# Input projection of a decoder step as seven block products over pairs of weight chunks, with intermediates in device memory

## The chip, the cores and the metric

The kernel runs on one core of one Trainium2 chip. Its engines are TensorE (PE, matrix products into PSUM), VectorE (DVE), ScalarE (ACT), GpSimd (POOL, which doesn't reach PSUM) and SyncE (SP, which here issues every DMA). Each engine works through a queue of its own in program order. The metric is the time of one execution on the device, in microseconds; less is better.

## The reference

One layer of a decoder trunk for a prompt of 1024 tokens and 8 sample tokens (1032 together), width 1024:

```
h = x * (1 + scale(c)) + shift(c)
z = h @ w_in                       # 1024 x 8704: 68 chunks of 128 columns
q, k, v, g_att | cb, cc, cx, g_conv | cu, cv, g_chunk | merge = split(z)
A = rms_norm(diff_attention(q, k, v)) * silu(g_att)       # 4 heads; samples attend to a paged cache
B = cb * conv3(cc * cx) * silu(g_conv)
C = cu * (tril(W_s) @ layer_norm(cv) + b) * silu(g_chunk)
sub = (sum_n sigmoid(merge_n) * (branch_n @ w_branch_n)) @ w_out
y = layer_norm(alpha * x + gate(c) * sub)
```

Outputs are y, the new keys and values, the tail of the convolution's input, and the normalised cv rows of the samples.

## The kernel before

Everything is kept transposed: channels on the 128 partitions, the 1032 tokens along the free axis. Each fp32 operand is held as two float32r parts, hi (a rounded copy, made by ACT) and lo (the remainder src - hi, made by DVE or POOL), and a product is three matmuls: hi*hi, hi*lo, lo*hi.

`gemm` (L235) makes one chunk of z: for each of three units of 344 tokens, 8 blocks of k times 3 matmuls go into one PSUM bank, and `evac` then takes the bank away. 

```python
for u, (a, b) in enumerate(UNITS):                 # L238: 3 units of 344 tokens
    for k in range(nk):                            # nk = 8 for z, 4 for a branch projection
        mm(ps[:, :n], wh, xh[k][:, a:b], k == 0, False)
        mm(ps[:, :n], wh, xl[k][:, a:b], False, False)
        mm(ps[:, :n], wl, xh[k][:, a:b], False, k == nk - 1)
    evac(u, a, b, ps[:, :n])
    tick()                                         # one more step of every background generator
```

`w_load` (L183) fetches weights as half chunks (128 x 512) and `w_split` (L194) splits each; the lo part goes to POOL during attention (`lo_eng[0] = pool`, L846) and to DVE from the merge of branch B on (L909). The rest of the model runs as Python generators that emit a few instructions at every `tick`, so that one instruction stream interleaves them with the projection: `attention(h)` (L384, one head each), `decode_k` (L668, scores of the samples over 128 cached pages of keys: POOL multiplies a 128x1024 tile `kp` by the query at L723, DVE sums it at L710 into `Sdec`), `decode_v` (L774, PE sums the 128 pages of values), `chunk_side` (L942), `rms` (L1057), `ada_gate` (L1095).

The order written out by hand is: `startup` (L577), where h arrives block by block and the chunks q, k, v of head 0 accumulate over k; for each head q, k, v and the four convolution chunks beside that head's attention; then the gates and projections of branch B beside `decode_k`; the chunk-mixing chunks; the gates and projections of branch C beside `decode_v`; the gates of branch A, g_att; the projections of branch A; the output projection (`out`). All activations stay in SBUF, in 43 slots of 128x1032.

Of the kernel before, what the change touches and what calls it, by code (L numbers as in the profile page):

```python
# [16 lines left out]
P = 128  # L17
# [5 lines left out]
UNITS = [(0, 344), (344, 688), (688, 1032)]  # L23
H = 4
# [40 lines left out]
def step_kernel(ctx, tc, cT, sm, sn, lamb, xT, x_p, x_s, ada, adag, bgate, w_in, w_br, w_out, lnb,  # L65
# [3 lines left out]
    NS = 43  # L69
    spool = ctx.enter_context(tc.tile_pool(name="S", bufs=NS))  # L70
    wpool = ctx.enter_context(tc.tile_pool(name="W", bufs=4))
    upool = ctx.enter_context(tc.tile_pool(name="U", bufs=4))
    cpool = ctx.enter_context(tc.tile_pool(name="C", bufs=1))
    mpool = ctx.enter_context(tc.tile_pool(name="M", bufs=4))
    pz = ctx.enter_context(tc.tile_pool(name="PZ", bufs=3, space=PSUM))
    px = ctx.enter_context(tc.tile_pool(name="PX", bufs=5, space=PSUM))
# [12 lines left out]
    def utile(name, dt=F32):  # L89
        return upool.tile([P, 344], dt, tag="U", name=name)  # L90
# [6 lines left out]

    active = []
    later = []

    def tick():
        todo, later[:] = later[:], []
        for f in todo:
            f()
        for g in list(active):
            try:
                next(g)
            except StopIteration:
                active.remove(g)

    def pause(n):
        for _ in range(n):
            yield
# [31 lines left out]
    kS = cpool.tile([P, H, NB], F32, name="kS")  # L145
    convo = cpool.tile([P, 4, 18], F32, name="convo")
    chko = cpool.tile([P, 4, NB], F32, name="chko")
    vS = cpool.tile([P, H, NB], F32, name="vS")
    pt = cpool.tile([1, NB * PAGES], I32, name="pt")

# [1 line left out]
    wseq = []  # L152

    def want(kind, c):
        wseq.extend([(kind, c, 0), (kind, c, 1)] if kind == "z" else [(kind, c, 0)])

    wseq.extend([("s", c, r) for r in range(2) for c in (C_Q, C_K, C_V)])
    for h in range(H):
        for b in (C_Q, C_K, C_V, C_CC, C_CX, C_GC, C_CB)[0 if h else 3:]:
            want("z", b + h)  # L160
    for n in (1, 2):
        if n == 2:
            for b in (C_CV, C_CU, C_GU):
                for g in range(4):
                    want("z", b + g)
        for d in range(KD):
            want("z", C_M + 8 * n + d)
            want("b", 8 * n + d)
    for c in (*range(C_M, C_M + 4), *range(C_GA, C_GA + 4), *range(C_M + 4, C_M + KD)):
        want("z", c)  # L170
    for d in range(KD):
        want("b", d)
        if d >= 1:
            wseq.extend([("o", d - 1, 0), ("o", d - 1, 1)])
    wseq.extend([("o", KD - 1, 0), ("o", KD - 1, 1)])
    woh, wol = {}, {}
    first = {c: [S.new(f"w0{x}{c}", F32R) for x in "hl"] for c in (C_Q, C_K, C_V)}
    wraw, wsp = {}, {}
    wpos = [0, 0, 0]
    proj_done = []  # L180
    lo_eng = [dve]

    def w_load():  # L183
        j = wpos[0]
        if j >= len(wseq):
            return
        wpos[0] += 1
        kind, c, r = wseq[j]
        t = wpool.tile([P, 512], F32, tag="raw", name=f"wr{j}", bufs=3)
        rc = slice(512 * r, 512 * r + 512)  # L190
        sp.dma_start(out=t, in_=w_br[c] if kind == "b" else (w_out if kind == "o" else w_in)[c, :, rc])
        wraw[j] = t

    def w_split():  # L194
        j = wpos[1]
        if j >= len(wseq):
            return
        kind, c, r = wseq[j]
        if kind == "o" and r == 0 and S.live + 4 > S.n and not proj_done:
            return  # L200
        wpos[1] += 1
        t = wraw.pop(j)
        if kind == "s":
            rc = slice(512 * r, 512 * r + 512)
            split(first[c][0][:, rc], first[c][1][:, rc], t, pool if j else dve)
            w_load()
            return
        if kind == "o":
            if r == 0:
                woh[c] = S.new(f"woh{c}", F32R)  # L210
                wol[c] = S.new(f"wol{c}", F32R)
            rc = slice(512 * r, 512 * r + 512)
            split(woh[c][:, rc], wol[c][:, rc], t)
            w_load()
            return
        hi = wpool.tile([P, 512], F32R, tag="hi", name=f"wh{j}")
        lo = wpool.tile([P, 512], F32R, tag="lo", name=f"wl{j}")
        split(hi, lo, t, lo_eng[0])
        wsp[j] = (hi, lo)
        w_load()  # L220

    def w_next(kind, c):
        parts = []
        while wseq[wpos[2]][0] in "os":
            wpos[2] += 1
        for r in range(2 if kind == "z" else 1):
            j = wpos[2]
            assert wseq[j] == (kind, c, r), (wseq[j], kind, c)
            wpos[2] += 1
            while wpos[1] <= j:  # L230
                w_split()
            parts.append(wsp.pop(j))
        return parts

    def gemm(kind, c, xh, xl, evac):  # L235
        parts = w_next(kind, c)
        nk = 4 * len(parts)
        for u, (a, b) in enumerate(UNITS):  # L238
            ps = pz.tile([P, 512], F32, tag="z", name=f"ps_{kind}{c}_{u}")
            n = b - a  # L240
            for k in range(nk):
                hi, lo = parts[k // 4]
                wh, wl = hi[:, (k % 4) * P:(k % 4 + 1) * P], lo[:, (k % 4) * P:(k % 4 + 1) * P]
                mm(ps[:, :n], wh, xh[k][:, a:b], k == 0, False)
                mm(ps[:, :n], wh, xl[k][:, a:b], False, False)
                mm(ps[:, :n], wl, xh[k][:, a:b], False, k == nk - 1)
                if nk == 8 and k == 3:
                    tick()
            evac(u, a, b, ps[:, :n])
            if len(wsp) + len(parts) < 4:  # L250
                w_split()
            tick()

# [13 lines left out]
    load_ada(0)  # L267
    w_load()
    load_x(0)
    load_ada(1)  # L270
    w_load()
    w_load()
    load_x(1)
    load_ada(2)
    load_x(2)
# [11 lines left out]
    hh, hl, parts_ = [], [], {}  # L287

    def ada_mm(k):
        ts = adr.pop(k)  # L290
        pa = xtile(f"pa{k}")
        for i, t in enumerate(ts):
            for kc in range(KD):
                j = 32 * (kc % 4)
                mm(pa[j:j + 32, i * P:(i + 1) * P], sct[:, kc * 32:(kc + 1) * 32],
                   t[:, kc * P:(kc + 1) * P], kc < 4 and i == 0, kc >= 4,
                   skip_group_check=True)
        S.free(2)
        part = utile(f"part{k}")
        act.copy(part[:, :256], pa[:, :256])  # L300
        parts_[k] = part

    def make_h(k):
# [8 lines left out]
        a = S.new(f"hh{k}", F32R)  # L312
        b = S.new(f"hl{k}", F32R)
        hf = S.new(f"hf{k}")
        for c in (slice(0, 512), slice(512, NP)) if k == 0 else (slice(0, NP),):
            act.activation(a[:, c], x[:, c], AF.Identity, bias=ss[:, 16:17], scale=ss[:, 0:1])
            dve.tensor_scalar(hf[:, c], x[:, c], ss[:, 0:1], ss[:, 16:17], ALU.mult, ALU.add)
            dve.tensor_tensor(b[:, c], hf[:, c], a[:, c], ALU.subtract)
        t8 = mtile(f"t8{k}", 8)
        dve.tensor_tensor(t8, x[:, NP:T], ss[:, 1:9], ALU.mult)  # L320
        dve.tensor_tensor(t8, t8, ss[:, 17:25], ALU.add)
        dve.tensor_copy(a[:, NP:T], t8)
        dve.tensor_tensor(b[:, NP:T], t8, a[:, NP:T], ALU.subtract)
        S.free()
        S.free()
        hh.append(a)
        hl.append(b)

# [1 line left out]
    st = {}  # L330

    def evac_q(h):
        q0 = S.new(f"Q0_{h}", F32R)
        q1 = S.new(f"Q1_{h}", F32R)
        st["Q", h] = (q0, q1)

        def f(u, a, b, ps):
            b2 = min(b, NP)
            n = b2 - a
            if n:  # L340
                act.copy(q0[0:64, a:b2], ps[0:64, :n])
                dve.tensor_tensor(q0[64:128, a:b2], ps[0:64, :n], q0[0:64, a:b2], ALU.subtract)
                act.copy(q1[64:128, a:b2], ps[64:128, :n])
                dve.tensor_tensor(q1[0:64, a:b2], ps[64:128, :n], q1[64:128, a:b2], ALU.subtract)
            if u == 2:
                dve.tensor_copy(qS[:, h, :], ps[:, n:n + NB])
        return f

    def evac_k(h):
        kf = S.new(f"kf{h}")  # L350

        def f(u, a, b, ps):
            act.copy(kf[:, a:b], ps)
            if u < 2:
                return
            later.append(lambda: sp.dma_start(out=kT_o[h], in_=kf))
# [27 lines left out]
    def attention(h):  # L384
# [16 lines left out]
        def scores(i, m):  # L401
            nk = (i + 1) * P
            if m:
# [3 lines left out]
                if i == 7:  # L407
                    S.free(7)
# [948 lines left out]
```

## Time and profile before

| | us |
|---|---|
| median of 3 runs | 1198.97 (1198.25 to 1199.39) |
| span of the profiled execution | 1197.8 |
| startup, to the first `ps_z` matmul | 61.7 |
| attention stage, 61.7 to 436.4 | 374.7 |
| products over the cached keys, 458.1 to 624.5 | 166.4 |
| products over the cached values, mostly 720 to 916 | about 200 |
| output projection, from 1092 | 97 |

The span is the time from the first to the last instruction of one profiled execution; the time of that execution by itself is not listed, and the median lies 1.2 above its span. A busy time is a union: overlapping records of one engine count once. Matmul records overlap (their ends are modelled), so the pace of PE is read from the starts of successive matmuls.

### The profile page before, as it was taken

Reading aid. Unit: us, or ns where it says so; the run is one execution under the profiler, and the core shown is the slowest. Engines: PE = TensorE matmul, PEld = TensorE weight load, DVE = VectorE, ACT = ScalarE, POOL = GpSimd, SP = SyncE. Lnnn points to the kernel's source line nnn. Section 1 sums busy time; section 2 is a strip of 40 time slices with the busy share of each in tenths; the row PEclk is TensorE's granted clock in tenths of the full one; section 3 lists DMA queues with packets and bytes.
Section 4 is the critical chain, followed back from the end, with each engine's and each line's share of the span. In section 5 each row is a group of like instructions: output and inputs, shape, how many; then the busy total and the mean of one; then the engine's idle time right before and its main releaser. Section 6 shows DMA issues by size and latency. Waiting matters only on the chain.

```text
span 1197.8 us, 20253 instructions
## 1 busy us (share of the span) xinstructions
PE 1180.9 (99%) x7599; PEld 1097.3 (92%) x7599; DVE 640.4 (53%) x1190; ACT 356.3 (30%) x709; POOL 381.8 (32%) x304
## 2 busy tenths in 40 slices
PE   7999999999999999999999999999999999999997
PEld 5799999999999999999999999888887899997785
DVE  5656547536625655777776775111211451197766
ACT  3344454343444342121224223111012232343000
POOL 2123222322322406999980001211211222254000
PEclk9999999999999999999999999999999999999999
DMA  9411110111111116777852234666674111133231
GB/s 358 184 63 37 49 59 29 43 71 37 36 53 63 36 46 208 248 249 234 259 186 65 75 106 140 230 216 223 215 244 158 54 44 45 46 119 120 89 106 53
DMA packets 73300, 146.62 MB, mean 122 GB/s; under 512 B 8409, under 2 KB 9306, under 8 KB 73202
## 3 DMA queue, kind: packets, MB, share of 16 engines
q1 hardware_dynamic: 73202, 145.34, 36.3%
q8 instruction: 59, 0.97, 0.3%
q14 instruction: 39, 0.32, 0.1%
HBM read 136.80 MB, written 8.51 MB: 121 GB/s over the span
## 4 chain that ended last, share of the span: by engine, by line
PE 95%; DVE 3%; DMA 1%; issue 0%; SPq 0%; POOL 0%; ACT 0%
PE ps_z L83 62%; PE ps_b L83 8%; PE out L83 8%; PE acc L83 3%; PE s L83 3%; PE dacc L83 3%; PE av L83 2%; PE t L461 1%; DVE wol L87 1%; DVE ml L1178 1%; DMA ada<-in_ada 1%; PE pa L83 1%; DVE wl L87 1%; PE mix L83 1%; PE cvt L952 0%
## 5 line engine op out<-in xcount | busy, mean ns | idle before, releaser
L83 PE MATMUL ps_z<-hh,wh 128*128 128x344 f32 x1560 | 509.3, 326 | 0.0
L83 PE MATMUL ps_z<-hh,wl 128*128 128x344 f32 x1560 | 498.8, 320 | 0.0
L83 PE MATMUL ps_z<-hl,wh 128*128 128x344 f32 x1560 | 498.3, 319 | 0.0
L83 PEld LDWEIGHTS ps_z<-hh,wh 128*128 128x128 f32 x1560 | 293.3, 188 | 25.8 <-issue 20.2
L83 PEld LDWEIGHTS ps_z<-hl,wh 128*128 128x128 f32 x1560 | 293.6, 188 | 1.5 <-issue 0.2
L83 PEld LDWEIGHTS ps_z<-hh,wl 128*128 128x128 f32 x1560 | 293.1, 188 | 0.2 <-DVE wl L87 0.2
L87 POOL TENSOR_TENSOR wl<-wr,wh 128x512 fp32r<-128x512 f32 x72 | 99.3, 1381 | 265.4 <-ACT wh L86 236.2
L723 POOL TENSOR_TENSOR kp<-kp,QB 128x1024 f32<-128x1024 f32 x64 | 162.0, 2563 | 12.3 <-DMA kp<-in_cache_k 11.4
L87 DVE TENSOR_TENSOR wl<-wr,wh 128x512 fp32r<-128x512 f32 x82 | 85.6, 1044 | 50.3 <-ACT wh L86 44.8
L710 DVE TENSOR_REDUCE Sdec<-kp 128x16 f32<-128x1024 f32 x64 | 77.4, 1213 | 37.8 <-POOL kp L723 37.8
L885 POOL TENSOR_TENSOR mg<-mg,sg 128x344 f32<-128x344 f32 x24 | 28.3, 1180 | 213.6 <-DVE sg L884 213.6
L83 PE MATMUL ps_b<-yh,wh 128*128 128x344 f32 x288 | 94.3, 328 | 0.4
L86 ACT CAST wh<-wr 128x512 fp32r<-128x512 f32 x154 | 93.2, 615 | 0.2
L83 PE MATMUL ps_b<-yl,wh 128*128 128x344 f32 x288 | 92.1, 320 | 0.0
L83 PE MATMUL ps_b<-yh,wl 128*128 128x344 f32 x288 | 92.1, 320 | 0.0
L901 ACT ACTIVATE sg<-ps_z 128x344 f32<-128x344 f32 x48 | 22.0, 458 | 213.3 <-PE ps_z L83 193.3
L437 ACT ACTIVATE E<-E,nb 128x128 f32<-128x128 f32 (+7 forms) x64 | 49.8, 777 | 112.3 <-DVE nb L436 107.0
L83 PEld LDWEIGHTS ps_b<-yh,wh 128*128 128x128 f32 x288 | 54.1, 188 | 11.5 <-issue 5.2
L884 DVE SCALAR_TENSOR_TENSOR sg<-sg,ps_b 128x344 f32<-128x344 f32 x24 | 12.3, 513 | 92.3 <-PE ps_b L83 89.1
L83 PEld LDWEIGHTS ps_b<-yl,wh 128*128 128x128 f32 x288 | 54.2, 188 | 0.1
L83 PEld LDWEIGHTS ps_b<-yh,wl 128*128 128x128 f32 x288 | 54.2, 188 | 0.0
L83 PE MATMUL out<-woh,ml 128*128 128x512 f32 (+1 forms) x136 | 51.9, 382 | 0.0
(285 smaller groups left out, 1518.2 us busy)
## 6 DMA issues: line engine op xcount, KB each, us to landing
wr<-in_w_in SPq DMA_DIRECT2D x136, 256.0 KB, 2.7
kp<-in_cache_k SPq DMA_DIRECT2D x128, 256.0 KB, 3.5
vp<-in_cache_v SPq DMA_DIRECT2D x128, 256.0 KB, 3.6
ada<-in_ada SPq DMA_DIRECT2D x16, 512.0 KB, 8.1
wr<-in_w_br SPq DMA_DIRECT2D x24, 256.0 KB, 2.6
xT<-in_xT SPq DMA_DIRECT2D x8, 516.0 KB, 9.7
adag<-in_adag SPq DMA_DIRECT2D x8, 512.0 KB, 5.7
wr<-in_w_out SPq DMA_DIRECT2D x16, 256.0 KB, 2.6
```

The lines of the kernel that those rows point to most:

```text
L83: pe.matmul(out, lhsT=lhsT, rhs=rhs, start=start, stop=stop, **kw)
L86: act.copy(hi, src)
L87: (eng or dve).tensor_tensor(lo, src, hi, ALU.subtract)
L437: act.activation(e[m], e[m], AF.Exp, bias=nb[:, m:m + 1], scale=SCALE, accum_out=su[:, m:m + 1])
L461: pe.transpose(ps[:, kb - lo, :], E[i][:, kb * P:(kb + 1) * P], ident)
L710: dve.reduce_sum(Sx[:, b, 2 * j:2 * j + 2, :], tiles.pop(i).rearrange("p e (a d) -> p e a d", d=DK), axis=AX.X)
L723: pool.tensor_tensor(t, t, q, ALU.mult)
L884: dve.scalar_tensor_tensor(sg[u], sg[u], 1.0, ps, ALU.add, ALU.mult)
L885: pool.tensor_tensor(merged[d][:, a:b], merged[d][:, a:b], sg[u], ALU.add)
L901: act.activation(sg[u], ps, AF.Tanh, scale=0.5)
L1178: dve.scalar_tensor_tensor(ml[d][:, a:b], m, 0.5, mh[d][:, a:b].bitcast(F32), ALU.mult, ALU.subtract)
```

## The change

Two chunks of z are made together. Their weights A (two chunks wide, 1024 deep) are cut into four blocks by chunk and by half of k, and h into four blocks by half of k and half of the tokens (516 each). Winograd's form of Strassen's scheme then gives the four blocks of the result from 7 products instead of 8. `prep` makes the sums of weight blocks (S1 to S4) and splits the seven left operands; `make_t` makes the sums of blocks of h (T1 to T4) once at the start; `pair` runs the seven products, each over 4 blocks of k and two units of 258 tokens, and adds up the results.

```diff
+    zpairs = [(C_V, C_Q + 1), (C_CC, C_CX), (C_GC, C_CB), (C_K + 1, C_V + 1),
...
+    zpairs += [(C_M + 8, C_M + 9), (C_M + 10, C_M + 11)]
+    zpairs += [(C_CV, C_CV + 1), (C_CV + 2, C_CV + 3)] + [(C_CU + g, C_GU + g) for g in range(4)]
+    zpairs += [(C_M + 8 * n + d, C_M + 8 * n + d + 1) for n in (1, 2, 0) for d in range(0, KD, 2)][2:]
...
+    def prep():
+        j, s = divmod(prepped[0], 7)
...
+        if s == 0:
...
+            parts[j, 0] = wsplit(A11, f"w{j}_0")
+            S1 = raw(f"S1_{j}")
+            s_eng[0].tensor_tensor(S1, A21, A22, ALU.add)
+            s_eng[0].tensor_tensor(A21, A11, A21, ALU.subtract)
+            s_eng[0].tensor_tensor(A11, S1, A11, ALU.subtract)
...
+        parts[j, s] = wsplit(wn[("S2", "A12", "S3", "S1", "A22", "A12")[s - 1]], f"w{j}_{s}")
+        if s == 2:
+            s_eng[0].tensor_tensor(wn["A12"], wn["A12"], wn["S2"], ALU.subtract)
...
+    def pair(c1_, c2_, e1, e2):
...
+        for s, (name, key, new) in enumerate((("B11", 0, True), ("T2", 1, True), ("B21", 0, False),
+                                              ("T3", 2, True), ("T1", 3, True), ("T4", 2, False),
+                                              ("B22", 3, False))):
+            while prepped[0] < min(7 * j + s + 3, 7 * len(zpairs)):
+                prep()
...
+            for u in range(2):
...
+                for i in range(4):
...
+                    mm(ps, wh, xh[:, c], new and i == 0, False, skip_group_check=True)
+                    mm(ps, wh, xl[:, c], False, False, skip_group_check=True)
+                    mm(ps, wl, xh[:, c], False, i == 3, skip_group_check=True)
+                a, b = QT * u, HT + QT * u
+                if s == 0:
+                    u2[u] = ztile(f"u2_{j}_{u}")[:, :QT]
+                    act.copy(u2[u], ps)
+                elif s == 1:
+                    dve.tensor_tensor(u2[u], ps, u2[u], ALU.add)
+                elif s == 2:
+                    e1(a, a + QT, ps, True)
+                elif s == 3:
+                    u3[u] = ztile(f"u3_{j}_{u}")[:, :QT]
+                    dve.tensor_tensor(u3[u], ps, u2[u], ALU.add)
+                elif s == 4:
+                    dve.tensor_tensor(u3[u], ps, u3[u], ALU.add)
+                    e2(b, b + QT, u3[u], False)
+                elif s == 5:
+                    z = ztile(f"z21_{j}_{u}")[:, :QT]
+                    dve.tensor_tensor(z, ps, u2[u], ALU.add)
+                    e2(a, a + QT, z, False)
+                else:
+                    dve.tensor_tensor(u2[u], ps, u2[u], ALU.add)
+                    e1(b, b + QT, u2[u], False)
+                tick()
...
+    def gate_out(dst):
+        def f(a, b, src, ps):
+            z = ztile("sg")[:, :QT] if ps else src
+            act.activation(z, src, AF.Tanh, scale=0.5)
+            store(dst[:, a:b], z)
+        return f
...
+    START = (1, 4, 7, 11, 16, 21, 28, 35)
...
     startup()
-    lo_eng[0] = pool
...
+    s_eng[0] = pool
+
+    def background():
+        yield from attention()
+        s_eng[0] = dve
+        yield from decode()
```

What else moves: the startup makes two chunks (q, k of head 0) instead of three, so 66 chunks in 33 pairs remain. `lo_eng` stays DVE throughout. PSUM is divided into 4 banks for `pair` and 4 for the rest (before 3 and 5). The blocks of h and the T's take 28 of the 43 slots while the pairs run, so q, the attention output, the convolution branch, cv, cu * silu, the chunk branch, silu(g_att) and the 24 gate chunks are stored to device memory by `store` (a DMA issued two ticks after the evacuation) and loaded again, and keys and values are read back from their outputs. Attention of the four heads, `decode_k` and `decode_v` form one chain of generators (51 ticks for a head, 5 ticks for 3 tiles of keys, 3 ticks for a step of values) beside the 462 ticks of the pairs, 14 to a pair; `chunk_side` starts when `decode_k` is done. All branch projections, in the order B, C, A, come after the pairs, with `rms` and then `ada_gate` beside them. The output projection stays as it was.

## Rows read from the trace of the kernel before

**Rows 1.** The page, part 1: busy us (share of the span) and instructions.
```profile
PE 1180.9 (99%) x7599; PEld 1097.3 (92%) x7599; DVE 640.4 (53%) x1190; ACT 356.3 (30%) x709; POOL 381.8 (32%) x304
```

**Rows 2.** The page, part 4: the chain that ended last, by engine.
```profile
PE 95%; DVE 3%; DMA 1%; issue 0%; SPq 0%; POOL 0%; ACT 0%
```

**Rows 3.** Busy time of each engine by stage, granted clock, DMA share and GB/s.
```profile
61.70:436.40 374.70, 374.70 (x2463) 371.09 (x2463) 207.83 (x527) 164.39 (x348) 111.19 (x117) 1.00 0.14 48
22.00:45.00 23.00, 23.00 (x216) 17.95 (x215) 15.41 (x34) 8.50 (x12) 6.22 (x14) 1.00 0.91 358
458.10:624.50 166.40, 166.40 (x1061) 165.94 (x1060) 125.44 (x115) 32.82 (x68) 161.57 (x65) 1.00 0.76 244
236.00:336.00 100.00, 100.00 (x659) 99.15 (x658) 50.94 (x130) 41.95 (x89) 29.86 (x31) 1.00 0.14 48
736.00:916.00 180.00, 180.00 (x1165) 148.13 (x1164) 25.89 (x48) 24.91 (x52) 31.74 (x27) 1.00 0.68 225
```

**Rows 4.** Groups of PE instructions by shape (busy us, mean ns).
```profile
L83 PE MATMUL ps_z<-hh,wh 128*128 128x344 f32 x1560 | 509.3, 326 | 0.0
```

**Rows 5.** The chain in order of time: start us, us, what.
```profile
497.52 11.33 PE ps_z L83 x72
...
26.31 1.60 PE acc L83 x6
...
28.26 2.88 PE acc L83 x12
...
34.09 2.88 PE acc L83 x12
```

**Rows 6.** Timeline of PE: first and last of 48 matmuls of 256 columns.
```profile
1183.11 0.28 PE L83 MATMUL out<-woh,mh 128*128 128x256 f32 x1
...
1188.63 0.28 PE L83 MATMUL out<-woh,ml 128*128 128x256 f32 x1
```

**Rows 7.** The tile `wl` (lo part of a weight half): duration min/median/max ns.
```profile
L87 DVE TENSOR_TENSOR wl<-wr,wh x82: 683/693/2467, 37.6 to 1083.7; 128x512 fp32r<-128x512 f32 x82
L87 POOL TENSOR_TENSOR wl<-wr,wh x72: 1280/1295/2151, 66.7 to 1041.1; 128x512 fp32r<-128x512 f32 x72
```

**Rows 8.** Timeline of DVE, two in a row; and one PSUM-fed shape by form.
```profile
648.32 0.69 DVE L87 TENSOR_TENSOR wl<-wr,wh 128x512 fp32r<-128x512 f32 x1 [2.83 <-ACT wh L86]
648.93 0.68 DVE L87 TENSOR_TENSOR wmr<-wm,wmr 128x512 fp32r<-128x512 f32 x1
...
L87 DVE TENSOR_TENSOR aT_l<-t,aT_h 128x256 fp32r<-128x256 f32 x8 | 3.4, 419 | 5.1 <-ACT aT_h L86 5.1
```

**Rows 9.** Groups of POOL and DVE in the stage of the cached keys, 453 to 613.
```profile
L723 POOL TENSOR_TENSOR kp<-kp,QB 128x1024 f32<-128x1024 f32 x60 | 152.2, 2568 | 12.3 <-DMA kp<-in_cache_k 11.4 <-DVE wl L87 0.7
L710 DVE TENSOR_REDUCE Sdec<-kp 128x16 f32<-128x1024 f32 x59 | 71.4, 1213 | 35.6 <-POOL kp L723 35.6
L87 DVE TENSOR_TENSOR wl<-wr,wh 128x512 fp32r<-128x512 f32 x27 | 42.3, 1566 | 0.4 <-ACT wh L86 0.4
L882 DVE SCALAR_TENSOR_TENSOR mg<-sg,ps_b 128x344 f32<-128x344 f32 x21 | 10.5, 499 | 6.5 <-PE ps_b L83 6.4
```

**Rows 10.** Timeline of DVE in that stage: a `wl` stands between the first two.
```profile
514.36 1.21 DVE L710 TENSOR_REDUCE Sdec<-kp 128x16 f32<-128x1024 f32 x1
...
517.17 1.21 DVE L710 TENSOR_REDUCE Sdec<-kp 128x16 f32<-128x1024 f32 x1
...
524.72 1.22 DVE L710 TENSOR_REDUCE Sdec<-kp 128x16 f32<-128x1024 f32 x1 [1.17 <-POOL kp L723]
527.08 1.22 DVE L710 TENSOR_REDUCE Sdec<-kp 128x16 f32<-128x1024 f32 x1 [1.14 <-POOL kp L723]
```

**Rows 11.** The tile `yc` (convolution taps, attention stage): duration min/median/max ns.
```profile
L545 DVE SCALAR_TENSOR_TENSOR yc<-p,snt,yc x12: 567/576/578, 79.5 to 394.5; 128x343 f32<-128x343 f32 x4, 128x344 f32<-128x344 f32 x4, 128x336 f32<-128x336 f32 x4
L547 DVE SCALAR_TENSOR_TENSOR yc<-p,snt,yc x12: 568/1607/1665, 80.1 to 395.1; 128x342 f32<-128x342 f32 x4, 128x344 f32<-128x344 f32 x4, 128x336 f32<-128x336 f32 x4
```

More of the change, by code (lines that the diff above doesn't have):

```diff
@@ L222, in w_next @@
[L222 to L252, printed above, removed]
@@ L659, in step_kernel @@
+            if pre:
+                try:
+                    next(pre)
+                except StopIteration:
+                    pre = False
+            yield
+        S.free(4)
+        if h + 1 < H and pre is not False:
+            while pre is None and ready[0] <= h:
+                yield
+            yield from pre or prelude(h + 1, nxt)
     dec = {}
-    vmax = [0]
     def pages(dst, cache, idx):
@@ new lines, in step_kernel, with b_split @@
+    yb = {}
+    bparts = {}
+    bpos = [0, 0]
+    woh, wol = {}, {}
+    proj_done = []
+    def b_split():
+        if bpos[0] >= len(bseq):
+            return
+        key = kind, c, r = bseq[bpos[0]]
+        if kind == "o" and r == 0 and S.live + 4 > S.n and not proj_done:
+            return
+        bpos[0] += 1
+        while key not in raws:
+            w_load()
+        t = raws.pop(key)
+        if kind == "o":
+            if r == 0:
+                woh[c] = S.new(f"woh{c}", F32R)
+                wol[c] = S.new(f"wol{c}", F32R)
+            rc = slice(512 * r, 512 * r + 512)
+            split(woh[c][:, rc], wol[c][:, rc], t)
+        else:
+            bparts[c] = wsplit(t, f"b{c}")
+        live[0] -= 1
+        pump()
@@ L942, in chunk_side, with load_y, load_sg @@
-    def chunk_side():
-        while not cv_done[0]:
-            yield
+    def load_y(n, src):
+        for k in range(4):
+            yield from need(1)
+            t = S.new(f"yl{n}_{k}")
+            sp.dma_start(out=t, in_=src[k])
+            yield from pause(2)
+            yb[n, k] = t
+    sgq = [(n, d) for n in (1, 2, 0) for d in range(KD)]
+    sgt = {}
+    def load_sg():
+        if sgq:
+            n, d = sgq.pop(0)
+            t = sgt[n, d] = S.new(f"sg{n}_{d}")
+            sp.dma_start(out=t, in_=gd[n, d])
@@ L945, in chunk_side @@
+    def chunk_side():
+        cvT = []
+        for g in range(4):
+            yield from need(1)
+            cvT.append(S.new(f"cvT{g}"))
+            sp.dma_start(out=cvT[g], in_=cvd[g])
+        yield from pause(3)
         mv = mpool.tile([P, 9, 2], F32, tag="mv", name="mv", bufs=1)
@@ L1184, in step_kernel @@
+    drain(sd)
     pend.pop()()
     proj_done.append(True)
-    while wpos[1] < len(wseq):
-        w_split()
+    while bpos[0] < len(bseq):
+        b_split()
+    while later:
+        tick()
     lng, lnbt = S.new("lng"), S.new("lnbt")
```

1155 lines of the change are left out of this document (637 added, 518 removed).

## The prediction

> **What bounds the kernel now.** I read the busy shares first: PE 99%, DVE about half [rows 1]. The chain of waits says the same, PE 95% of it [rows 2]. So every microsecond taken off PE counts, as long as no other engine becomes the later one. The stages tell how near the others are [rows 3]. In the attention stage DVE is busy 207.8 of 374.7 us. In the stage of the cached keys DVE is at 125.4 and POOL at 161.6 of 166.4 us. The granted clock stands at 1.00 in all of these. Elsewhere there is room: 25.9 us of DVE in 180 while the cached values are read.
>
> **The matmuls.** z now takes 65 chunks x 3 units x 24 = 4680 matmuls of 344 columns (three groups of 1560 [rows 4]); 72 of them follow each other in 11.33 us [rows 5], 157.4 ns each: 736.6 us. Afterwards it is 33 pairs x 7 products x 2 units x 12 = 5544 matmuls of 258 columns. The nearest row is 256 columns: 47 steps in 5.52 us [rows 6], 117.4 ns. With two columns more at (157.4 - 117.4)/88 = 0.45 ns this is 118.3 ns, 655.9 us in all. A fixed price per matmul that would eat the gain is excluded: both rows give 0.458 ns a column. **Gain 80.7 us.** A pair is 168 x 118.3 ns = 19.9 us, a tick 1.42 us. The Trainium skill (TensorE: Matmul & The Clock Gate, Back-to-back issue gap) gives N/2.4 + 2.5 ns, by estimate 110.0 and 145.8 ns here, and so a gain of 72.7 us, 8 us less; the trace differs from it (117.4 ns where the formula gives 109.2), and the rows decide.
>
> **Startup.** Per block of k, PE does 18 accumulating matmuls (2.88 + 1.60 us) in a period of 34.09 - 28.26 = 5.83 us [rows 5]. With 12, it can gain at most 1.5 us a block, 12 us. But every second block now also needs four sums on POOL, two ACT copies and two DVE subtractions of 1032 columns for the T's, and the loads stay. I take a third of it, **gain 4 us** (0 to 12).
>
> **What the pairs ask of DVE.** A 512-column subtraction takes 0.69 us, and two in a row start 0.61 apart [rows 8]. An add fed from PSUM is nearest to the 256-column row, 0.42 us, 0.34 with the same overlap [rows 8]. Each pair has seven lo parts (7 x 0.61), all on DVE now, and ten adds of 258 columns (3.4): 7.7 us of 19.9. ACT's share (seven copies beside evacuations) replaces what it did before and stays well below PE. Where attention is over, the four S sums come to DVE too (2.4).
>
> Whether an operation waits for POOL depends on where its inputs lie. In the stage of the cached keys, `wl`, with both inputs in SBUF, takes 1566 ns on average against 683 at best, while the reduction (1213 ns) and `mg`, which reads PSUM (499 ns), take what they take elsewhere [rows 7, 9]. POOL pays too: reductions that follow POOL's tiles are 2.36 us apart, 2.81 with one `wl` between [rows 10]. So POOL's two-input operations and DVE's exclude each other, at 0.45 us for POOL and 0.88 for DVE each time. The Trainium skill (SBUF — State Buffer, SBUF: two separate sides) says that of GpSimd and a Vector operation with two SBUF inputs the later one fully waits for the whole instruction of the other; by that rule an operation arriving at random would wait half of 2.36, 1.18 us, times POOL's share, and the stage below would come out some 12 us longer than by the row; the trace agrees with the rule in kind.
>
> **Stage of the cached keys: the decisive term.** By the steps counted in the code, attention starts after pair 0 and takes 215 ticks, so the 64 key tiles are emitted over ticks 233 to 339 of 462: 106 ticks, 7.6 pairs, 8.4 tiles a pair. PE needs 7.6 x 19.9 + 2 = 152 us there. DVE needs 64 reductions (1.13 each: 72), 53 lo parts and 30 S sums (0.61: 51), 76 adds (26), and for the four cu/g_chunk pairs 32 short products (11): 160 us, already more than PE. Of these 115 have both inputs in SBUF. *From below*: the two engines share the time, 64 x 2.36 = 151 on POOL plus 83 x 0.45 plus 32 x 0.25 = 196 us. *From above*: each of the 115 waits 0.88: 160 + 101 = 261 us. POOL holds 91% of the stage now and would hold 66% of a longer one, so the wait shrinks towards 0.64 (234 us). I take the middle of the bounds, 228 us: **loss 76 us** (44 to 109). PE waits because a PSUM pair of banks must be read within three units, 4.3 us, and DVE's queue is in order; behind the late adds stand the lo parts that the next product needs.
>
> **Attention stage.** 15.4 pairs. PE: 306 us plus what it does beside z now: 374.7 less 26 chunks at 11.33 = 80; together 386. DVE: 207.8 as before, plus 15.4 x 7.7 = 119, plus waits for POOL, which is busy 29.9 of 100 us there [rows 3] as before, since the S sums take the place of its lo parts. How such waits look stands in the second convolution tap: 1607 ns median where the first takes 576 [rows 11]. With a tenth to a third of that on some 110 added lo parts (10 to 35 us) DVE stands at 337 to 362 of 386, about 91%, in an in-order queue that also waits for ACT. Below: nothing, the queues absorb it. Above: half a microsecond for each of 100 lost ticks, 50 us. I take **loss 20 us**, nearer the lower end, as DVE is not over PE on average.
>
> **Device memory.** 52 tensors of 0.53 MB go out and come back, 55 MB more. It matters where the cached values are read: 33.5 MB in 101 ticks (150 us with PE's own share), 15 MB of weights and gates, 6 MB of chunk mixing: some 360 GB/s. Now PE is full there at 225 GB/s; the stretch at 22 to 45 us moved 358 [rows 3]. The value products stand in PE's queue, so a late page stops z. **Loss 6 us** (0 to 20). Stores wait in SP's queue for their evacuation, with weight loads behind; these are ordered most of a pair ahead and hidden, unless DVE is late, which is priced above.
>
> **The end.** 24 branch projections and the output projection keep their matmuls. The samples' attention ends about 15 to 25 ticks after the pairs; norm, gate and split of branch A then take some 25 ticks and stand just before that branch's projection at tick 510, with `ada_gate` behind: **loss 6 us** (0 to 25).
>
> **Sum.** -80.7 - 4 + 76 + 20 + 6 + 6 = +23.3 on the span of 1197.8, 1221; the median of the runs lies 1.2 above the span: **1222 us**.
>
> **The rivals.**
>
> *PE stays the bound but for the port (33%), faster.* DVE's two-input operations fall into POOL's gaps, since POOL, ahead by the tiles loaded in advance, runs dry when DVE is late. For it: in the trace DVE idles 35.6 us waiting for POOL's tiles, so its waits there cost PE nothing. Against: DVE then had 27 `wl` in the stage, now 83 with 32 more. The stage takes its lower bound (+44) and attention nothing: -80.7 - 4 + 44 + 12 = -28.7, **1170 us**. It decides the sign where the stage takes less than 228 - 23 = 205 us with the other terms as above.
>
> *Everything is hidden (8%), faster.* No engine but PE counts: -80.7 - 4, **1114 us**. DVE's own 160 us against PE's 152 in the keys stage speaks against it.
>
> *DVE bounds attention too (12%), slower still.* If each added lo part there meets POOL as the second tap does in 8 of 12 cases (0.69 us), 110 of them add 76 us: DVE 403 plus its waits for ACT against 386, and a loss near the 50 of the upper end: **1252 us**; with the keys stage at its upper end 1285.
>
> My own case keeps 47%.
>
> **How the numbers follow.** The case forecast has its own range of 1185 to 1265 (keys stage 44 to 109, others by half their bounds). Below it lie the two fast rivals, together 41%; above, the last one. The range that leaves out no more than 2 in 10 runs from 1135, under the port rival with startup and memory at their good ends (leaving most of the 8%), to 1275. A difference of 0.2%, 2.4 us, is about what a measurement of this kernel can tell from none. Faster takes the two fast rivals, 0.41; the lower tail of my case crosses no change, 0.05; slower 0.54.
>
> **What would show it.** Matmuls of 258 columns should follow each other at 118 ns wherever PE has no idle time. In the keys stage POOL should be busy about two thirds, PE about the same, DVE over 90%, `wl` well above 683 ns, and idle time of PE should end on DVE. During attention PE should be over 90% busy; the last seven pairs should take 20 to 22 us each. I am wrong if the keys stage lasts under 205 us, or if the attention stage, not this one, holds PE's idle time; if 258 columns take over 130 ns, the first term falls and everything turns slower.

## The result and the profile after

The changed kernel takes **1399.17 us** (median of 4 runs, 1398.15 to 1400.29) against 1199.18 (1198.25 to 1200.3) on the same chip: ratio 1.1666, 95% interval 1.1649 to 1.1682, slower by 16.7%. The forecast was 1222 with 1135 to 1275: the sign came out, the size did not. The profiled execution took 1400.29, its span is 1398.6.

The page after, part 1, to be read against [rows 1]:

```profile
PE 1192.8 (85%) x8397; PEld 1067.2 (76%) x8397; DVE 965.1 (69%) x1763; ACT 446.8 (32%) x919; POOL 409.1 (29%) x350
```

PE was busy 99% of a shorter span; now it is at 85%, and is busy for as many microseconds (1193 against 1181) although the products of z became cheaper. DVE has half as much work again. Busy time by stretch of the changed kernel (startup; pairs 0 to 16 with attention; pairs 17 to 24 with the cached keys; pairs 25 to 32 with the cached values and chunk mixing; the rest), columns as in [rows 3]: length, then busy us of PE, PEld, DVE, ACT, POOL, granted clock, DMA share, GB/s.

```profile
0.00:78.20 78.20, 49.01 (x416) 36.21 (x416) 43.31 (x77) 28.43 (x40) 39.12 (x58) 0.88 0.52 201
78.20:598.40 520.20, 458.38 (x3477) 439.74 (x3477) 352.91 (x835) 225.77 (x497) 140.75 (x151) 0.96 0.23 76
598.40:849.80 251.40, 189.12 (x1355) 182.29 (x1353) 235.75 (x263) 57.27 (x123) 166.80 (x68) 0.88 0.60 192
849.80:1117.10 267.30, 234.82 (x1685) 185.31 (x1685) 143.31 (x290) 79.93 (x166) 0.64 (x1) 0.95 0.64 207
1117.10:1398.60 281.50, 261.51 (x1468) 223.68 (x1468) 189.86 (x300) 55.43 (x95) 61.79 (x72) 0.99 0.47 168
```

Set beside the sum of the prediction (a pair at 19.9 us):

| stretch | by the prediction | measured | off |
|---|---|---|---|
| startup | 61.7 - 4 = 57.7 | 78.2 | +20.5 |
| pairs 0 to 16 | 17 x 19.9 + 80 + 20 = 438 | 520.2 | +82 |
| pairs 17 to 24 | 228 + 0.4 x 19.9 = 236 | 251.4 | +15 |
| pairs 25 to 32 and the end | 1221 less the above = 489 | 548.8 | +60 |

So the stage that I called decisive came out nearly as forecast. The forecast broke at the attention stage, priced at a loss of 20 us, at device memory and the end, priced at 6 us each, and at the startup, priced at a gain of 4.

The pace of the narrower matmuls is right. Timeline of PE in pair 0, 27 steps between these two starts, 119.6 ns each (forecast 118.3):

```profile
94.75 0.28 PE L87 MATMUL ps<-t13l,hw 128*128 128x258 f32 x1
...
97.98 0.28 PE L87 MATMUL ps<-t24l,hw 128*128 128x258 f32 x1
```

But the granted clock, 1.00 in all stages of [rows 3], is down to 0.88 to 0.96 until the pairs are done. It has two levels, 2.4 and 1.2 GHz. At 131.98, after 2.76 us without work, the same matmuls follow each other at 215 ns (132.33 to 134.48, ten steps):

```profile
128.93 0.28 PE L87 MATMUL s<-K,Qb 128*128 128x256 f32 x1
131.98 0.56 PE L87 MATMUL ps<-t24h,hw 128*128 128x258 f32 x1 [2.76 <-DVE u L314]
132.33 0.42 PE L87 MATMUL ps<-t24l,hw 128*128 128x258 f32 x1
...
134.48 0.42 PE L87 MATMUL ps<-t24h,lw 128*128 128x258 f32 x1
```

No term of the prediction held this. Counting the steps of z (from the start of one matmul of z to the next) between 150 and 250 ns gives 245 in pairs 0 to 16, 198 in the keys stage and 79 after it, some 90 ns too long each: 48 us. Beside them stand PE's plain gaps (length less busy time): 62 us in pairs 0 to 16, 62 in the keys stage, 32 in pairs 25 to 32.

### The profile page after: what moved, and what is told of

Its sections match the earlier page's. It is cut to its first block, busy times and chain, and to the rows that moved or that the text cites. A ratio compares the mean times of both kernels' runs of the same rounds, so it can differ in the third digit from the quotient of the medians.

```text
span 1398.6 us, 23794 instructions
## 1 busy us (share of the span) xinstructions
PE 1192.8 (85%) x8397; PEld 1067.2 (76%) x8397; DVE 965.1 (69%) x1763; ACT 446.8 (32%) x919; POOL 409.1 (29%) x350
## 5 line engine op out<-in xcount | busy, mean ns | idle before, releaser
L91 DVE TENSOR_TENSOR lw<-wr_z,hw 128x512 fp32r<-128x512 f32 x198 | 172.7, 873 | 100.8 <-ACT hw L90 92.6
L87 PE MATMUL ps<-t13h,hw 128*128 128x258 f32 x528 | 156.9, 297 | 18.2 <-DVE u L300 9.2
L87 PE MATMUL ps<-t24h,hw 128*128 128x258 f32 x528 | 155.4, 294 | 14.3 <-DVE u L314 12.3
L87 PE MATMUL ps<-hh,hw 128*128 128x258 f32 x528 | 155.3, 294 | 14.0 <-DVE u L307 10.9
L87 PE MATMUL ps<-t13h,lw 128*128 128x258 f32 x528 | 153.2, 290 | 7.2 <-DVE lw L91 7.2
L87 PE MATMUL ps<-hh,lw 128*128 128x258 f32 x528 | 152.4, 289 | 5.1 <-DVE lw L91 5.0
L87 PE MATMUL ps<-t13l,hw 128*128 128x258 f32 x528 | 152.0, 288 | 0.0
L87 PE MATMUL ps<-t24l,hw 128*128 128x258 f32 x528 | 151.4, 287 | 0.0
L87 PE MATMUL ps<-t24h,lw 128*128 128x258 f32 x528 | 151.2, 286 | 0.0
L87 PE MATMUL ps<-hl,hw 128*128 128x258 f32 x528 | 151.1, 286 | 0.0
```

The lines of the kernel that those rows point to most:

```text
L87: pe.matmul(out, lhsT=lhsT, rhs=rhs, start=start, stop=stop, **kw)
L91: (eng or dve).tensor_tensor(lo, src, hi, ALU.subtract)
```

## The experiments

Each run is one profiled execution of a changed version of the changed kernel, except the last of the mends, which was also timed. All are read by stretch. Pairs 1 to 16 alone take 496.6 us in the changed kernel. Runs that leave a stretch alone show how far it moves by itself: pairs 1 to 16 take 495.9 to 497.6 us in eight of them, pairs 17 to 24 take 250 to 255. The run on the startup, in which these pairs differ only in what their products read and in the slots that are free, has 508.0 and 243.6, so a difference of 12 us can come from a side effect.

**A pair without company.** Attention and the samples' attention are left out.

```diff
     def background():
+        yield from pause(2)
+        small_tables()
+        yield from pause(213)
+        s_eng[0] = dve
+        return
         yield from attention()
```

> Leaves out the whole background chain: attention of the prompt, scores and values of the samples (their results are replaced by other data); pairs, chunk mixing, projections and output stay. Theory A (the pair by itself keeps PE full; what stops it is the company on DVE, ACT and PSUM): the pairs come to 19.9 to 21 us each, 33 of them in about 670 us in place of 1039, granted clock 1.00 in that stretch, the run at 1030 us or less. Theory B (the pair's own chain, two products of preparation ahead and four banks, already stalls PE): 23 us or more a pair, PE idle at the pairs' own tiles, granted clock under 0.97, the run at 1130 us or more.

1065.31 us. The row of pairs 0 to 16:

```profile
77.30:432.50 355.20, 348.64 (x2860) 345.29 (x2861) 211.87 (x403) 112.63 (x239) 111.44 (x115) 1.00 0.27 86
```

Most pairs take 20.1 us; the four that carry the gate of the convolution take 22.7. The clock stands at 1.00. So preparation, four banks and the adds of the scheme keep PE full by themselves, and theory A holds for them. The whole run ends 35 us above its figure: pairs 23 to 26, beside chunk mixing, took 28 to 34 us each, so the 33 pairs came to 724 us and not to 670.

**The stage of the cached keys.** Three runs: without POOL's products, without DVE's reductions (ACT makes small copies instead), and with the products on DVE.

```diff
-            pool.tensor_tensor(t, t, q, ALU.mult)                      # first run: deleted
+            dve.tensor_tensor(t, t, q, ALU.mult)                       # third run
-            dve.reduce_sum(Sx[:, b, 2 * j:2 * j + 2, :], ...)          # second run
+            act.copy(Sx[:, b, 2 * j:2 * j + 2, :], t[:, :, 0:8])
```

> Leaves out POOL's 64 products of the cached keys by the query; DVE still adds up the 64 tiles. Theory port: without POOL's two-input operations DVE's 160 us of work fit beside PE's 165, and the stage of the keys falls from 251 us to 170 to 185, with lw back at about 0.7 us each. Theory load (DVE has more work there than PE, whatever POOL does): the stage stays at 215 or above and lw stays above 0.8 us. The other stages stay as they are.

> The counterpart: POOL multiplies the 64 key tiles as before, but DVE's 64 reductions (72 us) are replaced by copies of 16 columns on ACT. Theory port: POOL's products and DVE's 115 two-input operations still exclude each other, and the stage of the keys takes 190 to 215 us, longer than without the products. Theory load: 165 to 180 us, as short as or shorter than without the products.

> The products of the cached keys are made by DVE instead of POOL, nothing is left out; result as the reference's. DVE gets 64 two-input operations of 1024 columns, by twice the 0.61 us of 512 columns about 1.2 us each, 78 us more, and no operation of POOL is left to exclude its own. Theory port: DVE's operations cost what they cost elsewhere, and DVE's 160 us become 238, so the stage of the keys takes 235 to 255 us, no longer than with POOL's help, though POOL's 166 us of work moved to the engine that is latest. Theory load: the stage grows by most of the 78 us, to 300 or more.

For each the stage (pairs 17 to 24, busy time by window), then groups of instructions in it. The changed kernel, whose stage row stands above:

```profile
L894 POOL TENSOR_TENSOR kp<-kp,QB 128x1024 f32<-128x1024 f32 x64 | 166.0, 2610 | 79.1 <-DMA kp<-in_cache_k 48.8 <-DVE Sdec L881 16.2 <-DVE u L627 8.8
L881 DVE TENSOR_REDUCE Sdec<-kp 128x16 f32<-128x1024 f32 x62 | 74.5, 1206 | 0.0
L91 DVE TENSOR_TENSOR lw<-wr_z,hw 128x512 fp32r<-128x512 f32 x47 | 63.2, 1344 | 4.1 <-ACT hw L90 4.1
```

Without the products:

```profile
596.40:786.30 189.90, 172.26 (x1356) 167.79 (x1353) 166.63 (x263) 57.38 (x123) 0.82 (x4) 0.97 0.78 246
```

```profile
L91 DVE TENSOR_TENSOR lw<-wr_z,hw 128x512 fp32r<-128x512 f32 x47 | 32.1, 682 | 5.7 <-ACT hw L90 5.6
```

Without the reductions:

```profile
596.50:828.30 231.80, 178.30 (x1355) 175.38 (x1353) 193.54 (x202) 64.36 (x184) 166.22 (x68) 0.89 0.66 208
```

```profile
L91 DVE TENSOR_TENSOR lw<-wr_z,hw 128x512 fp32r<-128x512 f32 x47 | 74.0, 1574 | 22.4 <-ACT hw L90 22.0
```

With the products on DVE:

```profile
597.30:851.80 254.50, 190.16 (x1355) 179.69 (x1353) 237.55 (x326) 57.25 (x123) 0.82 (x4) 0.92 0.60 189
```

```profile
L894 DVE TENSOR_TENSOR kp<-kp,QB 128x1024 f32<-128x1024 f32 x64 | 77.9, 1218 | 1.8 <-DMA kp<-in_cache_k 1.8
...
L91 DVE TENSOR_TENSOR lw<-wr_z,hw 128x512 fp32r<-128x512 f32 x47 | 32.1, 683 | 3.6 <-ACT hw L90 3.4
```

Taking POOL's products away saves 61.5 us of the stage, 0.96 us for each; `lw`, the lo part of a weight operand, falls from 1344 ns to 682, the reductions stay at 1.21 us. Taking away some 72 us of DVE's own work saves 20, and `lw` grows to 1574. That decides against load, for the exclusion, though 189.9 lies 5 us above what theory port had named and 231.8 above what either had. The last run shows it best: DVE does POOL's 64 products too, in 77.9 us, `lw` is back at 683 ns although DVE has more to do, and the stage is as long as with POOL (254.5 against 251.4). POOL's 166 us of help buy 3 us, no more than this stage moves by itself.

The stage at 189.9 is still 29 us above the 161 of PE's work (8 pairs at 19.9 and 2 us more, by the prediction's own figures): DVE is busy 166.6 of it. In the changed kernel PE's idle time in the stage ends on DVE, as forecast; the largest item of PE's waits from 598 to 850 us (who waits for whom: total us, times, longest) is the add that empties a bank:

```profile
PE ps L87 <- DVE z L311: 38.6, 8, 7.4
```

**The low clock in that stage.** Three matmuls of 254 columns more in each unit, into unused columns of its bank.

```diff
+                for _ in range(fill[0]):      # 3 while the keys are worked on
+                    mm(acc[key, u][:, QT:512], wh, xh[:, 0:512 - QT], False, False, skip_group_check=True)
```

> While the cached keys are worked on, each unit gets three more matmuls of 254 columns into the unused columns of its bank (some 106 units, 318 matmuls, 38 us at 0.12 each). Theory that DVE and POOL set the pace there and the low clock is only a consequence of PE's waits: the stage stays within 10 us of 251, and its granted clock rises from 0.88 to 0.94 or more. Theory that PE's work at the low clock sets the pace: the stage takes 275 us or more.

1400.75 us. The stage:

```profile
596.60:852.00 255.40, 216.59 (x1682) 212.62 (x1680) 235.04 (x263) 57.65 (x123) 165.86 (x68) 0.94 0.59 189
```

The stage has 327 more matmul records, some 39 us at 0.12 each, and is 4 us longer, no more than it moves by itself. The low clock in this stage is a consequence of PE's waits and sets no pace there.

**Attention: sums, depth, head start.** Three runs took work away or prepared further ahead, and one (the second) moved the sums of weight blocks to DVE.

```diff
-            S1 = raw(f"S1_{j}")                                        # no sums, in prep()
-            s_eng[0].tensor_tensor(S1, A21, A22, ALU.add)
-            s_eng[0].tensor_tensor(A21, A11, A21, ALU.subtract)
-            s_eng[0].tensor_tensor(A11, S1, A11, ALU.subtract)
...
-    s_eng[0] = pool                                                    # sums on DVE
...
-            while prepped[0] < min(7 * j + s + 3, 7 * len(zpairs)):    # one product more ahead
+            while prepped[0] < min(7 * j + s + 4, 7 * len(zpairs)):
...
-        at(START[3] + 2, q_next)                                       # K, Q, V of head 0
...
-                pre = prelude(h + 1, nxt)
```

> Leaves out the four sums of weight blocks of each pair (the products then take the blocks themselves). Theory port (operations with two SBUF inputs on POOL and DVE exclude each other): in the attention stage POOL loses 64 sums of 1.24 us, and DVE gets back up to 0.88 us for each, so the stage falls from 520 us to 465 or so; the stage of the cached keys loses 30 sums of DVE, 0.61 to 0.9 us each, and falls from 251 to 225 to 233. Theory latency (PE waits for single late operations in the in-order queues, not for DVE's or POOL's sum of work): attention stays above 500, keys above 240.

> The changed kernel with the sums of weight blocks on DVE throughout: in the attention stage 64 two-input operations of 1.24 us leave POOL, and DVE gets 64 of 0.61 us, 39 us on 353 of 520. Theory port: POOL's sums hold DVE up by more than they cost there, and the pairs 1 to 16 fall from 497 by 5 to 24 us (24 is what leaving them out gave). Theory load: a longer DVE queue makes them 10 us or more longer. The other stages stay.

> One more buffer for hi and one for lo, and each product prepared three products ahead in place of two (the short tiles get 12 buffers in place of 16 to make the room). Theory depth: late hi and lo parts are what stops PE; the attention stage falls from 520 us to 490 or less, and the stage of the keys from 251 to 235 or less. Theories head start and port: PE waits for the evacuation of its PSUM banks and for attention's own operands, which come no earlier; both stages stay within 10 us of what they are.

> Heads 1 to 3 leave out their own keys, queries and values: they use the tiles K, V and Q of head 0, and no head makes Q for its second half (rows 512 on use Q of the first half). Scores, softmax, transposes and products stay as many. Theory head start (the attention stage loses its time where a head begins or turns to its second half, since K, Q and V are rebuilt there in one burst on ACT and DVE): the pairs 5, 6, 9, 10, 12, 13 and 14, now 33, 35, 28, 38, 35, 29 and 41 us, come to 25 to 28, and the stage falls from 520 us to 455 to 470. Theory depth (PE stops wherever the small rows of attention hold ACT's and DVE's in-order queues, since a pair is prepared only two products ahead): the stage stays above 490.

| run | pairs 1 to 16 | pairs 17 to 24 | whole run |
|---|---|---|---|
| changed kernel | 496.6 | 251.4 | 1400.29 |
| no sums | 473.5 | 220.2 | 1338.57 |
| sums on DVE | 508.3 | 250.6 | 1409.14 |
| one product more ahead | 504.1 | 261.0 | 1411.06 |
| K, Q, V of head 0 for all heads | 472.3 | 250.9 | 1372.35 |

The sums cost 23 us in attention, which puts the stage between its two theories, and 31 in the keys stage, where they are DVE's. Moved to DVE in attention they cost 12 more, which may be a side effect. That doesn't clear the exclusion: by the traces DVE is busy 344 us in pairs 1 to 16, 318 without the sums, and 362 with them on DVE, 46 of these for the sums themselves. So on POOL the sums hold DVE's other work up by some 26 us, only 4 of them at `lw`, and made by DVE they take more than that. Whether the 23 us come from this or from sums that are late isn't shown. One product more ahead doesn't help (its 12 short buffers may have cost something). Rebuilding K, Q and V costs 24, less than half of what theory head start wanted: with pair 0 the stage takes 496.2, above the 490 of theory depth. Since depth itself gave nothing, what is left of that theory is the held queue: an instruction that waits keeps back what stands behind it on its engine.

**Attention: the held queue.** The trace of the changed kernel, ACT around 250 us (start, us, what; in brackets the idle time before and what ended it), then DVE and PE behind it:

```profile
248.00 0.62 ACT L90 CAST hw<-wr_z 128x512 fp32r<-128x512 f32 x1
253.27 0.40 ACT L741 ACTIVATE E<-E,nb 128x128 f32<-128x128 f32 x1 [4.65 <-DVE nb L740]
...
253.67 0.60 ACT L90 CAST hw<-wr_z 128x512 fp32r<-128x512 f32 x1
```

```profile
253.08 0.15 DVE L740 TENSOR_SCALAR nb<-mx 128x1 f32<-128x1 f32 x1
254.30 0.69 DVE L91 TENSOR_TENSOR lw<-wr_z,hw 128x512 fp32r<-128x512 f32 x1 [1.07 <-ACT hw L90]
254.91 0.42 DVE L311 TENSOR_TENSOR z<-ps,u 128x258 f32<-128x258 f32 x1
```

```profile
255.48 0.47 PE L87 MATMUL ps<-b,hw 128*128 128x258 f32 x2 [1.67 <-DVE z L311]
```

ACT stands 4.65 us at an exponential whose bias `nb` DVE makes only at 253.08; `hw` stands behind it, DVE's `lw` waits for `hw`, the add that empties the bank stands behind `lw`, and PE waits for that bank 1.67 us. So the exponentials were issued one tick later than their scores, first together with two other mends, then alone.

```diff
-            act.activation(e[m], e[m], AF.Exp, ...)      # in scores(i, m)
+        def expo(i, m):                                  # the same activation
...
+            at(t + 1, expo, i, 0)
+            at(t + 2, expo, i, 1)
```

> The exponentials are issued one tick later than the scores that they follow; Q is made in two steps, two ticks apart, with three more ticks ahead of the rows 512 on; chunk mixing waits ten ticks for its loads in place of three. The result is the reference's. Theory held queue (ACT stands at an exponential whose bias DVE has not made yet, 156 us in all, with hi parts and evacuations behind it): ACT's wait for nb falls below 60 us, the pairs 1 to 16 fall from 497 us together to 455 or less although attention has 16 ticks more, and pair 27 from 46 to 35; the run at 1345 or less. Theory port or load: the pairs 1 to 16 stay above 485, the run above 1375.

> Only the exponentials one tick later; Q, ticks and chunk mixing as in the changed kernel. The result is the reference's. Theory held queue: this alone brings the pairs 1 to 16 from 497 us to 470 or less, with ACT's wait for nb under 80 us (156). Theory burst of Q: they stay above 485, and PE's waits for Qa and for the banks behind it (some 20 us) are still there.

> The run before with late exponentials gained 52 us in the pairs 1 to 16 and 16 in pair 27, and gave 46 back after the pairs, since its 20 more ticks of attention pushed the samples' attention into the projections. Here the ticks are those of the changed kernel: exponentials one tick late, Q made in two steps one tick apart, chunk mixing waits ten ticks for its loads. The result is the reference's. Theory held queue: the pairs 1 to 16 take 460 us or less (497), what follows the pairs 290 or less, the run 1335 or less. Rival: it was the three ticks of room ahead of row 512 that helped; then the pairs 1 to 16 take 475 or more, and the run 1350 or more.

The view of waits, 78 to 600 us, of the changed kernel, then of the exponentials alone (L744 is the same activation):

```profile
ACT E L741 <- DVE nb L740: 155.9, 64, 6.6
DVE lw L91 <- ACT hw L90: 74.9, 55, 3.2
```

```profile
ACT E L744 <- DVE nb L740: 77.4, 40, 6.6
...
DVE lw L91 <- ACT hw L90: 38.8, 37, 2.5
```

Both waits halve, PE's gaps in pairs 1 to 16 fall from 62 us to 37, and these pairs fall to 464.0 by this alone (run 1366.85). With Q in two steps they come to 460.0 and pair 27 to 31.8 (run 1347.94, of which 1335 was expected: pairs 25 to 32 gained 11 rather than 16). With more ticks for attention (20, not the 16 that its expectation counted) they came to 445.0, but the samples' attention ended later, and the stretch after the pairs grew from 281.5 to 327.7 (run 1357.13). The held queue is shown as the largest of the causes taken apart here, 33 us.

**Startup.** T1 to T4 and their splits left out; products take blocks of h.

```diff
-        t = (t13 if name in ("T1", "T3") else t24)[i]                  # in hblock()
+        if name in ("T1", "T3"):
+            return b11[i][:, 0, :], b11[i][:, 1, :]
+        c = slice(0, HT) if name == "T2" else slice(HT, T)
+        return hh[4 + i][:, c], hl[4 + i][:, c]
```

> Leaves out the sums T1 to T4 of blocks of h and their splits; the products take the blocks of h themselves. To be read for the startup alone. Theory T: the sixteen operations on POOL, eight copies on ACT and eight subtractions on DVE stand in the way of the splits of h and of the first weights, and the first pair starts at 61 to 67 us in place of 78. Rival: the loads and the splits of h set it; it starts at 74 or later.

```profile
0.00:62.30 62.30, 45.10 (x416) 33.20 (x416) 25.35 (x69) 21.25 (x32) 11.11 (x42) 1.00 0.66 252
```

Startup takes 62.3 us, as long as before the change (61.7): the T's cost 16 us, and a third less of accumulating matmuls gave nothing.

**Beside the cached values.** The products of the values, by form, before and after:

```profile
L83 PE MATMUL dacc<-vp,Sdec 128*8 128x512 f32 x256 | 33.4, 594 | 0.0
```

```profile
L87 PE MATMUL dacc<-vp,Sdec 128*8 128x512 f32 x256 | 56.5, 618 | 10.3 <-DMA vp<-in_cache_v 10.2
```

The same matmuls take 33 us more, idle time included: pages come one by one while PE stands in the middle of a group. The transfer rate (207 GB/s) is no higher than the 225 before the change [rows 3]. Of SP's waits in 850 to 1117 the three longest are:

```profile
SPq L124 <- ACT u L546: 22.8, 11, 7.4
SPq L124 <- ACT z L546: 18.3, 6, 5.5
SPq L124 <- ACT sg L546: 10.8, 6, 4.8
```

Line 124 is a store, 546 the activation that makes a gate: SP stands 52 us at gates that ACT has not made, with page loads behind. Four runs, the last two with as many bytes as the changed kernel:

> Chunk mixing starts after the last pair instead of beside the cached values, so that up to 13 slots of activations stay free there; result as the reference's. In the changed kernel the 32 groups of value products last 61.8 us together, 28.6 more than at 1.04 each, since pages land late. Theory slots: the loads are issued late because the 43 slots are full (28 hold the blocks of h); with the slots free the groups' excess falls under 6 us and the pairs 25 to 32 from 267 us to 215 or less; the end takes longer by what mixing needs. Theory queue or bandwidth: the gates' stores stand ahead of the pages in SP's queue or share the transfer engines; the excess stays above 18 us.

> Leaves out the 48 stores of gates and their 24 loads (the gates of the projections are zeros). Theory queue or bandwidth: the excess of the value products falls from 28.6 us to under 10, and the end, where gates are loaded, is 10 us or more shorter. Theory slots: the excess stays above 18 us, the pairs 25 to 32 stay above 255 us, and the end changes by less than 8 us.

> The gates' 48 stores are issued by ACT, right behind the activation that makes the piece, instead of by SP two ticks later; as many bytes move. Theory queue (SP stands at a store whose piece ACT has not made, and the page loads stand behind it): the value products' excess falls from 28.6 us to under 10, the pairs 25 to 32 from 267 to 245 or less, the run to about 1375. Theory bandwidth (the stores share the transfer engines with the pages): the excess stays above 20 us and the pairs above 258.

> The gates' stores stay with SP but are issued four ticks after their evacuation instead of two. Theory queue: SP finds the pieces made and no longer waits; the excess falls from 28.6 us to 15 or less. Theory bandwidth: it stays above 22 us, and nothing else changes.

```diff
-        if j >= 23 and "S" in dec and mx not in active and not mixed:  # mixing after the pairs
+        if j >= 99 and "S" in dec and mx not in active and not mixed:
...
-            store(dst[:, a:b], z)                        # in gate_out; deleted: no gate stores
+            act.dma_start(out=dst[:, a:b], in_=z)        # by ACT
+            store(dst[:, a:b], z, 4)                     # or: by SP, two ticks later
```

| run | value products beyond 1.04 us a group | pairs 25 to 32 | after the pairs | whole run |
|---|---|---|---|---|
| changed kernel | 28.6 | 267.3 | 281.5 | 1400.29 |
| mixing after the pairs | 24.8 | 228.7 | 362.0 | 1441.0 |
| no gate stores or loads | 6.2 | 234.7 | 274.2 | 1359.51 |
| stores by ACT | 10.3 | 251.4 | 279.7 | 1384.38 |
| stores later | 19.2 | 253.3 | 284.1 | 1387.34 |

In the first column the excess over 1.04 us (what a group of 8 takes without a wait) is added up over the 32 groups. Free slots don't bring the pages earlier: theory slots falls. Without gate traffic pairs 25 to 32 lose 32.6 us; the end loses 7, less than the 10 named. With the same bytes but the stores out of SP's way, or later in it, they lose 16 and 14, so about half is SP's queue; the other half went only where the stores were left out, and whether their bytes or their issue cost it isn't shown. The last two runs came out between their theories.

**The mends together**, timed: late exponentials, Q in two steps, ten ticks for chunk mixing's loads, stores by ACT.

> The mends together: exponentials one tick late, Q in two steps, ten ticks for chunk mixing's loads (1348 us by themselves), and the gates' stores issued by ACT. Theory queue: 1318 to 1332 us. Theory bandwidth: 1340 to 1350. By all theories still slower than the kernel before, since the stage of the cached keys (250 us where PE needs 165) and the startup stay as they are.

1338.93 us (median of 4 runs, 1336.18 to 1340.43) against 1199.82: ratio 1.1158 (95% interval 1.114 to 1.1177). 60 us come back, between what the two theories had named. No version that leaves nothing out comes near the kernel before.

## Why the prediction was right or wrong

**The matmuls: right.** 119.6 ns for 118.3; 20.1 us for a pair alone, 19.9 forecast.

**The stage of the cached keys: right in mechanism, 15 us small.** The stretch took 251 for 236, and DVE was busy 94% of it, as forecast; POOL 66%, as forecast. The wait of a lo part was put at 0.64 us for a stage of that length; `lw` waits 1344 - 682 ns, 0.66. By that wait DVE had 234 us to do, and it was busy 236. The 228 was the middle of two bounds, so part of the nearness is luck. The Trainium skill (SBUF — State Buffer, SBUF: two separate sides) calls the shared port pair an exclusive lock; the three runs agree in kind, since DVE doing all of POOL's products is no slower.

**The attention stage: the step that failed.** I argued "the queues absorb it", "as DVE is not over PE on average", and took 20 us of 0 to 50. Pairs 1 to 16 took 496.6 where 16 x 19.9 + 80 is 398. DVE was busy 353 of 520 us: the amount was forecast rightly (337 to 362), but it is 68% of the stage, far below the 91% that I had feared, so a sum of busy time could not show the loss. What counts is order: an instruction that waits for another engine holds all behind it. Before the change ACT waited for `nb` too, but in this stage 49 of the 51 lo parts of weights were POOL's, and their wait for a late hi part (`wh` there) cost PE nothing: it was busy for the whole stage [rows 3]. The view of waits of the kernel before, 61 to 437 us:

```profile
POOL wl L87 <- ACT wh L86: 144.1, 33, 10.7
ACT E L437 <- DVE nb L436: 107.0, 56, 5.3
```

Now a late `hw` holds DVE, and DVE holds the banks of z. The Trainium skill (TensorE: Matmul & The Clock Gate, the table ahead of Part 1) gives ScalarE and VectorE strictly ordered queues; the 4.65 us above agree. Shown: 33 us by the exponentials, 24 by the rebuilding of K, Q and V, 23 by the sums' presence (these overlap and don't add). After the mends 460 remain against 398. By the trace of the run at 460.0, 34 us of PE's gaps and 13 us of slow steps of z stand in it; and without company these 16 pairs took 332 us where 16 x 19.9 is 318, most of it beside the gate of the convolution. What causes the gaps that remain stays open, and whether the low clock costs anything here by itself wasn't tried.

**Device memory: the second failed step.** I wrote 6 us, and that stores in SP's queue were "hidden, unless DVE is late". It was ACT's gates that were late, and behind them stood not only weights but the pages. Gate traffic cost 33 us beside the values, about half of it by SP's queue, and perhaps 7 at the end. Chunk mixing's own reload, which had no price of its own, added to this: PE waited 13 us for the stored cv, gone with ten ticks in place of three.

**Startup: wrong in sign.** "I take a third of it, gain 4" set the saved matmuls against the T's without adding these up; they cost 16 us and the saving was nothing.

**The end: 6 forecast.** It took 262 us with no attention beside it at all and 281.5 with the samples' attention, 19 us: 13 more than taken, inside its bounds of 0 to 25.

**The bounds.** My upper end took each term's upper end for unlikely with the others. But attention and memory failed together, both by queues that wait in order, the startup failed beside them, and where PE had gaps its clock fell too, which no term priced. Of the signs that I named, two came out against me: attention holds as much of PE's idle time as the keys stage (62 us each), with PE busy 88% of it and not over 90%, and the last seven pairs took 22 to 46 us and not 20 to 22.

## What to carry to other kernels

When a change gives an engine more instructions in a stage with cross-engine chains, don't stop at busy time against the bound: for each instruction that waits on another engine, write down what stands behind it on its queue, and whether the bound engine needs that within its buffers' reach. Issue such a waiter one step later than its producer; here that one move gave 33 us. A helper engine whose operations and those of the engine it helps exclude each other may be worth next to nothing (3 us here); test it by moving its work over, not only by taking it away.

## What the runs showed of the hardware that I had not expected

POOL multiplying 64 tiles (166 us busy) beside DVE made the stage hardly shorter (251.4 us) than DVE doing it alone in 78 us (254.5). Where PE waits, 327 matmuls more were free within 4 us and raised the granted clock from 0.88 to 0.94. Right behind a gap of 2.76 us PE's matmuls stood 215 ns apart in place of 120.
